# Two-layer hybrid decoder trunk: [high | low] products in the first SwiGLU phase, modulation steps moved to the first mixer, half of the depthwise conv on GpSimd

## The chip, the cores and the metric

The kernel runs on one core of a Trainium2 chip. The metric is device time in microseconds (us) of one execution; lower is better. Engines are called as in the profile: PE is the matrix engine, PEld its weight loads, DVE the vector engine, ACT the scalar engine, POOL is GpSimd, and SP issues most DMAs.

## The reference

Two layers work on x of 256 positions by 1024 channels, all in float32. A vector c gives nine modulation vectors of 1024 per layer.

```python
for l in range(2):
    mod = silu(c) @ ada_w[l] + ada_b[l]           # 1024 -> 9 * 1024
    sh1, sc1, gt1, sh2, sc2, gt2, sh3, sc3, gt3 = split(mod, 9)
    h = rms(x) * (1 + sc1) + sh1
    x = x + 0.5 * gt1 * swiglu(h, ffn1_w_in[l], ffn1_w_out[l])      # 1024 -> 2 * 2816 -> 1024
    P = (rms(x) * (1 + sc2) + sh2) @ mix_w_in[l]
    # attention (8 heads of 64), conv branch, gated linear attention (4 heads of 64)
    o_b = silu(group_layernorm(depthwise_conv31(a * sigmoid(g)) + b))   # 256 channels, causal
    x = x + gt2 * (concat(o_a, o_b, o_c) @ mix_w_out[l])
    h = rms(x) * (1 + sc3) + sh3
    x = x + 0.5 * gt3 * swiglu(h, ffn2_w_in[l], ffn2_w_out[l])
```

## The kernel before

Everything is kept transposed: channels on the 128 partitions, the 256 positions along the free axis. The program is a sequence of phases, named (layer, sub-layer): (0,0), (0,1), (0,2), (1,0), (1,1), (1,2). Sub-layers 0 and 2 are the SwiGLUs (`ffn`), 1 is the mixer (`mix`). A scheduler orders each engine's instructions when the program is built; on the chip each engine runs its list in order.

**Weights.** Each weight piece is 1 MB. `split` loads it into one of five `raw` buffers, ACT copies it to a rounded high part `wh`, and DVE subtracts to get the low part `wl` (lines 327 and 328); there are six buffers each of `wh` and `wl`, of 1024 columns. The activations are held as a high and a low part too: `hT` has both side by side, and `g` (the SwiGLU's inner result) is built the same way.

**Two forms of a product.** Per 128x128 weight block, `mm3` issues three matmuls of 256 columns: high weights by high activations, high weights by low, low weights by high. `mm2` issues two: high weights by the pair [high | low] in one matmul of 512 columns, and low weights by high. `product` uses `mm3` and leaves its sum in one bank of PSUM for both halves of a piece. `product2` uses `mm2`, needs one bank per half, and adds the two column halves outside PE: an ACT copy (line 524) and a DVE addition (line 525) per half. In `ffn` the flag `pairs` selects `product2` in all SwiGLU phases but (0,0). Of the 22 input pieces of (0,0), three are done in `open_first` and 19 by `product`; each has 16 blocks.

**Modulation.** `ada_w` is 72 loads of 1 MB. A step takes one of them: in mode "dve", DVE multiplies it by a column of silu(c) and accumulates (lines 230, 232); in mode "pe", PE multiplies it directly (line 223). When the eight steps of a group of 16 vectors of 128 are done, `ada_sum` adds over partitions on PE (line 251), and `ada_finish` transposes (line 263), adds the bias and forms the scale and gate columns. `PLAN[phase] = (m, tensor, lo, hi)` spreads m steps over the pieces lo to hi of a phase; `AT_END[phase]` adds steps in mode "pe" near the phase's end. Modulation loads share the five `raw` buffers with the weights, and SP issues both from one queue. The opening of (0,0) does the first eight steps; the groups that follow are 16 to 31 (gate 1, shift 2), 32 to 47 (scale 2, gate 2) and 48 to 63 (shift 3, scale 3).

**Conv.** `conv_steps` in `mix` is a generator: each `yield` follows one of the 31 taps, and `taps(n)` is called between the steps of the attention so that the taps lie between other DVE work. A tap is one DVE instruction for each 128 channels (t = 0, 1), accumulating into `y` (lines 732, 735). When all taps are done, a matmul (line 740) begins the group norm. The two POOL memsets of `acaus` (line 898) come later in program order.

`unit` hands out one of 24 buffers of 2 KB per partition, from which most activations come.

Of the kernel before, what the change touches and what calls it, by code (L numbers as in the profile page):

```python
# [44 lines left out]
TAPS = (4, 2, 4, 4, 4, 4)  # L45
ORDER = (0, 2, 6, 4)

PLAN = {None: (0, 0, 0, 1), (0, 0): (22, 0, 0, 30), (0, 1): (0, 0, 0, 1), (0, 2): (19, 0, 5, 28), (1, 0): (15, 0, 5, 28),
        (1, 1): (0, 0, 0, 1), (1, 2): (4, 0, 2, 14)}
AT_END = {(0, 0): 1, (0, 1): 1, (0, 2): 1, (1, 0): 1, (1, 1): 0, (1, 2): 0}  # L50
HOOKS = {(0, 1): (0, 1), (0, 2): (0, 1), (1, 0): (0, 1), (1, 1): (0, 1), (1, 2): (0, 1)}
# [8 lines left out]
def trunk_kernel(ctx: ExitStack, tc: tile.TileContext, x, c, positions, ada_w, ada_b, ffn1_norm, ffn1_w_in,  # L60
# [487 lines left out]
    def ffn(l, i, w_in, w_out, done, first=None):  # L548
# [2 lines left out]
        gT = []  # L551
        ws = []

        pairs = (l, i) != (0, 0)

        def piece(n, ahead=0):

            while len(ws) <= min(n + ahead, KF - 1):
                m = len(ws)
                ws.append(split(wi[:, :, m % 2, T * (m // 2):T * (m // 2) + T], [KD, T], fine=m < 2))  # L560
            return ws[n]
# [14 lines left out]
        for ch in range(KF // 2):  # L576
            if (l, i) == (0, 0) and ch in (2, 6):
                next(tables_rope)
            if (l, i, ch) == (0, 2, 3):
                use_small(1, *load_small(1))  # L580
            if first is not None and ch < 2:
                if ch == 0:
                    continue
                pb = product(piece(3))
                opened, bias = first[4:]
                b = bias()
                for s in range(2):
                    act(opened[0][:, s, :], opened[0][:, s, :], AF.Silu, bias=b[:, s:s + 1])
                    DVE.scalar_tensor_tensor(opened[0][:, s, :], opened[1][:, s, :], b[:, 2 + s:3 + s],
                                             opened[0][:, s, :], op0=ALU.add, op1=ALU.mult)  # L590
                gated(opened[0])
                a = opened[2]
                for s in range(2):
                    act(a[:, s, :], a[:, s, :], AF.Silu, bias=b[:, 4 + s:5 + s])
                DVE.tensor_mul(a, a, pb)
            elif ch == 0:
                (a, ba), (b, bb) = rms(pps[0]), rms(pps[1])
                wh, wl = piece(2)
                pp = [wide(), wide()]
                for k in range(KD):  # L600
                    for s in range(2):
                        cs = P * s, P * s + P
                        mm3(pp[s][:, 0:T + 2], wh(k, *cs), wl(k, *cs), hT[:, k, 0, :], hT[:, k, 1, :], k == 0,
                            k == KD - 1)
                third = rms(pp)
                piece(3)
                modulated(l, i)
                for s in range(2):
                    act(a[:, s, :], a[:, s, :], AF.Silu, bias=ba[:, s, :])
                    DVE.scalar_tensor_tensor(a[:, s, :], b[:, s, :], bb[:, s, :], a[:, s, :], op0=ALU.add,  # L610
                                             op1=ALU.mult)
            else:
                if ch == 1:
                    a, ba = third
                    for s in range(2):
                        act(a[:, s, :], a[:, s, :], AF.Silu, bias=ba[:, s, :])
                elif pairs:
                    a = product2(piece(2 * ch))
                    act(a, a, AF.Silu)
                else:  # L620
                    a = unit([P, 2, T], F32, "ab")
                    act(a, product(piece(2 * ch)), AF.Silu)
                DVE.tensor_mul(a, a, (product2 if pairs else product)(piece(2 * ch + 1)))  # L623
            gated(a)
        wo = w_out[l].rearrange("(k p) n -> p k n", p=P)
        late = []
# [50 lines left out]
    def mix(l, done):  # L677
# [47 lines left out]
        def conv_steps():  # L725

            y = tv
            for k in range(CK):
                for t in range(2):
                    w = cw[l][:, 2 * k + t:2 * k + t + 1]  # L730
                    if k == 0:
                        DVE.tensor_scalar(y[:, t, :], hpad[:, t, 0:T], w, cols[l][:, R_CB + t:R_CB + t + 1],
                                          op0=ALU.mult, op1=ALU.add)
                    else:
                        DVE.scalar_tensor_tensor(y[:, t, :], hpad[:, t, k:k + T], w, y[:, t, :], op0=ALU.mult,  # L735
                                                 op1=ALU.add)
                yield
            pm = bank()
            for t in range(2):
                PE.matmul(pm[:, T * t:T * t + T], grpb, y[:, t, :], start=True, stop=True)  # L740
            DVE.tensor_sub(y, y, pm.rearrange("p (a b) -> p a b", a=2))
            ACT.activation(tg, y, AF.Square)
            bc = group_rstd(tg)
            DVE.tensor_mul(y, y, bc)
            table("silu_and_others")
            for t in range(2):
                act(y[:, t, :], y[:, t, :], AF.Silu, scale=cols[l][:, R_CG + t:R_CG + t + 1],
                               bias=cols[l][:, R_CBE + t:R_CBE + t + 1])
                split_out(y[:, t, :], mixed(4 + t))
            yield  # L750
# [408 lines left out]
```

## Time and profile before

| what | value |
|---|---|
| median of 3 runs | 1063.79 us (1062.51 to 1064.71) |
| the profiled execution, its own time | 1062.44 us |
| its span in the trace | 1060.6 us |
| PE busy | 1043.7 us, 98% of the span |
| DVE / ACT / POOL busy | 855.6 / 600.5 / 6.6 us |
| bytes moved | 251.36 MB, 237 GB/s in the mean |

The profiled execution lasts 1.84 us longer than its span; the median of the runs is 1.35 us above it. A busy share is an average over phases that have different limits, and since PE's matmuls are pipelined, a busy PE is not yet a PE at its peak; rows of single stretches are needed to see what sets the time.

### The profile page before, as it was taken

How to read it: one execution, taken by the hardware profiler on the slowest of the kernel's cores; microseconds unless marked ns; L12 is line 12 of the kernel's file. 1: busy time of each engine (PE TensorE's matmuls, PEld its weight loads, DVE VectorE, ACT ScalarE, POOL GpSimd, SP SyncE). 2: the span in 40 equal slices, each digit the busy share in tenths (PEclk: the TensorE clock that was granted, in tenths of full speed). 3: DMA queues.
4: the chain of work that ended last, by engine and by line, in shares of the span. 5: the costliest groups of instructions: out<-in, count | busy, mean ns of one | idle time of the engine just before them, and what ended most of it. 6: DMA issues, size and time to landing. Idle time of an engine off the chain costs nothing.

```text
span 1060.6 us, 17714 instructions
## 1 busy us (share of the span) xinstructions
PE 1043.7 (98%) x6987; PEld 919.3 (87%) x6987; DVE 855.6 (81%) x1430; ACT 600.5 (57%) x1067; POOL 6.6 (1%) x30
## 2 busy tenths in 40 slices
PE   5999999999999999999999999999999999999998
PEld 4799998888888988888889888888988899888887
DVE  3698887979986899998669998865899789976552
ACT  5464454458665865555457565544767577555541
POOL 1000000000000000000000000000000000000000
PEclk8999999999999999999999999999999999999999
DMA  9989999995326469999776998867343436965430
GB/s 315 366 305 353 328 311 310 318 304 170 125 75 207 152 225 344 346 345 328 239 236 200 321 345 297 284 221 237 122 158 120 159 97 226 311 202 172 159 127 20
DMA packets 177587, 251.36 MB, mean 237 GB/s; under 512 B 7372, under 2 KB 156512, under 8 KB 170336
## 3 DMA queue, kind: packets, MB, share of 16 engines
q1 hardware_dynamic: 177272, 250.14, 70.2%
q8 instruction: 55, 0.90, 0.4%
q14 instruction: 28, 0.23, 0.1%
q10 hardware_dynamic: 232, 0.09, 0.0%
HBM read 249.16 MB, written 1.05 MB: 236 GB/s over the span
## 4 chain that ended last, share of the span: by engine, by line
PE 97%; DMA 1%; DVE 1%; ACT 0%; issue 0%; ACTq 0%; DVEq 0%
PE mm L353 36%; PE mm L354 18%; PE mm L347 8%; PE mm L349 7%; PE mm L348 7%; PE mm L702 3%; PE mm L701 2%; PE mm L703 2%; PE mm L954 2%; PE mm L955 2%; PE mm L953 1%; PE tp L223 1%; PE tp L859 1%; PE tp L832 1%; PE tp L251 1%; PE tp L854 1%
## 5 line engine op out<-in xcount | busy, mean ns | idle before, releaser
L328 DVE TENSOR_TENSOR wl<-raw,wh 128x1024 fp32r<-128x1024 f32 (+1 forms) x352 | 391.8, 1128 | 103.0 <-ACT wh L327 97.8
L327 ACT CAST wh<-raw 128x1024 fp32r<-128x1024 f32 (+1 forms) x352 | 338.5, 975 | 186.3 <-PE mm L353 100.3
L353 PE MATMUL mm<-hT,wh 128*128 128x512 f32 x912 | 322.5, 396 | 0.0
L354 PE MATMUL mm<-hT,wl 128*128 128x256 f32 x912 | 256.0, 281 | 0.0
L353 PE MATMUL mm<-g,wh 128*128 128x512 f32 x704 | 249.3, 398 | 0.0
L353 PEld LDWEIGHTS mm<-hT,wh 128*128 128x128 f32 x912 | 172.3, 189 | 43.0 <-DVE ab L525 1.7
L354 PE MATMUL mm<-g,wl 128*128 128x256 f32 x704 | 197.6, 281 | 0.0
L347 PE MATMUL mm<-hT,wh 128*128 128x256 f32 (+1 forms) x656 | 187.3, 286 | 1.7 <-ACT hT L432 1.5
L349 PE MATMUL mm<-hT,wl 128*128 128x256 f32 (+1 forms) x656 | 187.1, 285 | 0.0
L348 PE MATMUL mm<-hT,wh 128*128 128x256 f32 (+1 forms) x656 | 186.8, 285 | 0.0
L354 PEld LDWEIGHTS mm<-hT,wl 128*128 128x128 f32 x912 | 171.6, 188 | 0.2
L353 PEld LDWEIGHTS mm<-g,wh 128*128 128x128 f32 x704 | 132.2, 188 | 34.9 <-ACT wh L327 1.7
L354 PEld LDWEIGHTS mm<-g,wl 128*128 128x128 f32 x704 | 133.0, 189 | 0.0
L347 PEld LDWEIGHTS mm<-hT,wh 128*128 128x128 f32 x656 | 124.7, 190 | 5.2 <-ACT hT L432 2.1
L349 PEld LDWEIGHTS mm<-hT,wl 128*128 128x128 f32 x656 | 124.8, 190 | 1.7 <-issue 1.6
L232 DVE SCALAR_TENSOR_TENSOR adaacc<-adaraw,cact,adaacc 128x2048 f32<-128x2048 f32 (+1 forms) x59 | 123.4, 2092 | 2.7 <-DMA adaraw<-in_ada_w_dram 2.6
L348 PEld LDWEIGHTS mm<-hT,wh 128*128 128x128 f32 x656 | 124.5, 190 | 0.7 <-DVE hT L433 0.2
L524 ACT COPY ab<-mm 128x256 f32<-128x256 f32 x114 | 41.7, 371 | 57.5 <-PE mm L354 57.3
L673 ACT CAST g<-ab 128x256 fp32r<-128x256 f32 x88 | 31.7, 404 | 39.5 <-DVE ab L623 39.2
L525 DVE TENSOR_TENSOR ab<-ab,mm 128x256 f32<-128x256 f32 x114 | 46.0, 415 | 9.0 <-ACT ab L524 8.7
L735 DVE SCALAR_TENSOR_TENSOR ab<-hpad,cw,ab 128x256 f32<-128x256 f32 x120 | 50.9, 475 | 0.0
L530 DVE SCALAR_TENSOR_TENSOR xT<-mm,gate,xT 128x256 f32<-128x256 f32 x80 | 34.5, 478 | 19.1 <-PE mm L354 18.8
(216 smaller groups left out, 1110.8 us busy)
## 6 DMA issues: line engine op xcount, KB each, us to landing
raw<-in_ffn_w_in_dram SPq DMA_DIRECT2D x85, 1024.0 KB
adaraw<-in_ada_w_dram SPq DMA_DIRECT2D x72, 1024.0 KB
raw<-in_ffn_w_out_dram SPq DMA_DIRECT2D x32, 1024.0 KB
raw<-in_mix_w_in_dram SPq DMA_DIRECT2D x24, 1024.0 KB
raw<-in_ffn_w_out_dram SPq DMA_DIRECT2D x16, 768.0 KB
raw<-in_mix_w_out_dram SPq DMA_DIRECT2D x8, 1024.0 KB
held<-in_ffn_w_in_dram SPq DMA_DIRECT2D x12, 256.0 KB
xn<-in_x_dram SPq DMA_DIRECT2D x4, 256.0 KB
```

Of the source, the lines that this page charges most:

```text
L232: DVE.scalar_tensor_tensor(part, w, cact[:, k, 0:1], part, op0=ALU.mult, op1=ALU.add)
L327: ACT.copy(hs[-1][:, b:c], raw_at(a + b, a + c))
L328: DVE.tensor_sub(ls[-1][:, b:c], raw_at(a + b, a + c), f32(hs[-1][:, b:c]))
L347: PE.matmul(o, wh, high, start=first, stop=False)
L348: PE.matmul(o, wh, low, start=False, stop=False)
L349: PE.matmul(o, wl, high, start=False, stop=last)
L353: PE.matmul(halves(o), wh, pair, start=first, stop=False)
L354: PE.matmul(o[:, 0:T], wl, pair[:, 0, :], start=False, stop=last)
L524: ACT.copy(t[:, s, :], o[s][:, T:2 * T])
L525: DVE.tensor_add(t[:, s, :], t[:, s, :], o[s][:, 0:T])
L530: DVE.scalar_tensor_tensor(xT[:, d, :], o, gate[l][i][:, d:d + 1], xT[:, d, :], op0=ALU.mult, op1=ALU.add)
L735: DVE.scalar_tensor_tensor(y[:, t, :], hpad[:, t, k:k + T], w, y[:, t, :], op0=ALU.mult, op1=ALU.add)
```

## The change

There are three edits. (1) The phase (0,0) uses `product2` everywhere; `pairs` is gone. (2) The plan of (0,0) has 16 steps in place of 22, and that of (0,1), the first mixer, has 6 in mode "dve" over its pieces 1 to 12; `AT_END` is as before, so the totals at the end of (0,1) agree. (3) In both mixers the taps of the second 128 channels go to POOL, which issues a multiplication into `term` and an addition for each tap; all of them stand in program order at the first tap. `term` is one more buffer from `unit`.

```diff
-PLAN = {None: (0, 0, 0, 1), (0, 0): (22, 0, 0, 30), (0, 1): (0, 0, 0, 1), (0, 2): (19, 0, 5, 28), ...
+PLAN = {None: (0, 0, 0, 1), (0, 0): (16, 0, 0, 30), (0, 1): (6, 0, 1, 12), (0, 2): (19, 0, 5, 28), ...
...
-        pairs = (l, i) != (0, 0)
...
-                pb = product(piece(3))
+                pb = product2(piece(3))
...
-                elif pairs:
+                else:
                     a = product2(piece(2 * ch))
                     act(a, a, AF.Silu)
-                else:
-                    a = unit([P, 2, T], F32, "ab")
-                    act(a, product(piece(2 * ch)), AF.Silu)
-                DVE.tensor_mul(a, a, (product2 if pairs else product)(piece(2 * ch + 1)))
+                DVE.tensor_mul(a, a, product2(piece(2 * ch + 1)))
...
         def conv_steps():
             y = tv
-            for k in range(CK):
-                for t in range(2):
-                    w = cw[l][:, 2 * k + t:2 * k + t + 1]
-                    if k == 0:
-                        DVE.tensor_scalar(y[:, t, :], hpad[:, t, 0:T], w, cols[l][:, R_CB + t:R_CB + t + 1],
-                                          op0=ALU.mult, op1=ALU.add)
-                    else:
-                        DVE.scalar_tensor_tensor(y[:, t, :], hpad[:, t, k:k + T], w, y[:, t, :], op0=ALU.mult,
-                                                 op1=ALU.add)
+            def tap(k, t):
+                return hpad[:, t, k:k + T], cw[l][:, 2 * k + t:2 * k + t + 1]
+            for t, V in ((0, DVE), (1, POOL)):
+                V.tensor_scalar(y[:, t, :], *tap(0, t), cols[l][:, R_CB + t:R_CB + t + 1], op0=ALU.mult, op1=ALU.add)
+            term = unit([P, 2, T], F32, "term")
+            for k in range(1, CK):
+                POOL.tensor_scalar(term[:, k % 2, :], *tap(k, 1), None, op0=ALU.mult)
+                POOL.tensor_add(y[:, 1, :], y[:, 1, :], term[:, k % 2, :])
+            yield
+            for k in range(1, CK):
+                DVE.scalar_tensor_tensor(y[:, 0, :], *tap(k, 0), y[:, 0, :], op0=ALU.mult, op1=ALU.add)
                 yield
```

## Rows read from the trace of the kernel before

**Rows 1.** The page's busy shares, and its chain that ended last.

```profile
PE 1043.7 (98%) x6987; PEld 919.3 (87%) x6987; DVE 855.6 (81%) x1430; ACT 600.5 (57%) x1067; POOL 6.6 (1%) x30
...
PE 97%; DMA 1%; DVE 1%; ACT 0%; issue 0%; ACTq 0%; DVEq 0%
```

**Rows 2.** PE's waits over the whole span, longest first: total us, times, longest.

```profile
PE mm L1055 <- DMA xn<-in_x_dram: 3.6, 2, 3.4
...
PE tp L1099 <- DVE shift L1092: 1.0, 1, 1.0
```

**Rows 3.** Busy time by stretch: stretch, length, PE, PEld, DVE, ACT, POOL, PE clock, DMA.

```profile
425.70:476.50 50.80, 50.80 (x290) 44.15 (x288) 49.12 (x61) 29.43 (x51) 0.00 (x0) 1.00 1.00 350
51.00:160.00 109.00, 109.00 (x913) 108.03 (x911) 96.43 (x122) 58.12 (x88) 0.00 (x0) 1.00 0.94 322
...
246.00:327.00 81.00, 81.00 (x523) 67.86 (x522) 76.60 (x179) 54.14 (x111) 0.00 (x0) 1.00 0.41 133
...
762.00:843.00 81.00, 81.00 (x542) 67.55 (x541) 75.75 (x183) 53.97 (x110) 0.00 (x0) 1.00 0.45 145
```

**Rows 4.** The stretch of three-matmul products, line 349 alone (PE, PEld).

```profile
57.35:126.48 69.13, 54.28 (x192) 36.17 (x192) 1.00 0.96 331
```

**Rows 5.** Stretches of two-matmul products, line 353 alone (PE, PEld).

```profile
162.46:188.90 26.44, 26.39 (x76) 14.10 (x76) 1.00 0.94 309
390.77:419.17 28.40, 28.36 (x80) 15.12 (x80) 1.00 0.94 330
...
425.65:476.56 50.91, 50.87 (x144) 27.19 (x144) 1.00 0.99 349
```

**Rows 6.** Groups by form, whole span: count, busy us, mean ns, idle before.

```profile
L232 DVE SCALAR_TENSOR_TENSOR adaacc<-adaraw,cact,adaacc 128x2048 f32<-128x2048 f32 x45 | 105.5, 2345 | 2.5 <-DMA adaraw<-in_ada_w_dram 2.5
...
L525 DVE TENSOR_TENSOR ab<-ab,mm 128x256 f32<-128x256 f32 x114 | 46.0, 415 | 9.0 <-ACT ab L524 8.7
L524 ACT COPY ab<-mm 128x256 f32<-128x256 f32 x114 | 41.7, 371 | 57.5 <-PE mm L354 57.3
```

**Rows 7.** Line 232 alone in a stretch of (0,0): DVE busy and count.

```profile
51.00:160.00 109.00, 28.14 (x12) 1.00 0.94 322
```

**Rows 8.** PE in order of time at the end of phase (0,2): start, us.

```profile
542.68 1.04 PE L251 MATMUL tp<-adaacc,ones 128*32 128x512 f32 x8
...
548.29 0.28 PE L354 MATMUL mm<-g,wl 128*128 128x256 f32 x1
548.41 0.28 PE L347 MATMUL mm<-hT,wh 128*128 128x258 f32 x1
```

**Rows 9.** DVE in order of time, first mixer: taps, and the operation before line 820.

```profile
248.34 0.73 DVE L732 TENSOR_SCALAR ab<-hpad,cw,cols 128x256 f32<-128x256 f32 x2
...
266.54 0.42 DVE L815 TENSOR_TENSOR tmp<-tmp,tmp 128x256 f32<-128x256 f32 x1
...
307.80 4.42 DVE L735 SCALAR_TENSOR_TENSOR ab<-hpad,cw,ab 128x256 f32<-128x256 f32 x11
```

**Rows 10.** PE in order of time, first mixer: lines 820 and 740.

```profile
267.01 0.66 PE L820 MATMUL tp<-ident,tmp 128*128 128x128 f32 x4
...
337.10 1.13 PE L740 MATMUL tp<-ab,grpb 128*128 128x256 f32 x4
```

**Rows 11.** POOL in order of time.

```profile
3.22 0.30 POOL L125 TENSOR_SCALAR_AFFINE_SELECT gmask<-gmask 128x128 f32<-128x128 f32 x1
3.45 0.53 POOL L129 MEMSET reset<- 128x512 f32 x1
...
226.84 0.99 POOL L898 MEMSET acaus<- 128x512 f32 x2 [221.49 <-PE mm L354]
```

**Rows 12.** Groups of DVE in the first mixer, 246 to 327 us.

```profile
L328 DVE TENSOR_TENSOR wl<-raw,wh 128x1024 fp32r<-128x1024 f32 x23 | 27.5, 1216 | 0.0
L735 DVE SCALAR_TENSOR_TENSOR ab<-hpad,cw,ab 128x256 f32<-128x256 f32 x60 | 25.4, 474 | 0.0
```

**Rows 13.** SP's DMA issues in order of time, first mixer.

```profile
254.10 2.62 SPq L312 DMA_DIRECT2D raw<-in_mix_w_in_dram  x2
```

More of the change, by code (lines that the diff above doesn't have):

```diff
@@ L46 @@
 ORDER = (0, 2, 6, 4)
-PLAN = {None: (0, 0, 0, 1), (0, 0): (22, 0, 0, 30), (0, 1): (0, 0, 0, 1), (0, 2): (19, 0, 5, 28), (1, 0): (15, 0, 5, 28),
+PLAN = {None: (0, 0, 0, 1), (0, 0): (16, 0, 0, 30), (0, 1): (6, 0, 1, 12), (0, 2): (19, 0, 5, 28), (1, 0): (15, 0, 5, 28),
         (1, 1): (0, 0, 0, 1), (1, 2): (4, 0, 2, 14)}
```

## The prediction, made before the change was run

> **What bounds the kernel now.** I read the page's shares first, then PE's waits, then the busy time by stretch. PE is busy for 98% of the span, and the chain that ended last is 97% PE [rows 1]. A busy PE could still be waiting inside that figure, so the second view asks whom it waits for: the longest wait is 3.6 us, for x to arrive at the start, and the next one on the page that the argument meets is 1.0 us, still in the opening [rows 2]. After that PE waits for nobody by more than a fraction of a microsecond, at a granted clock of 1.00, which is the 2.4 GHz level [rows 3]. So time can leave this kernel only where PE gets less to do, and it can enter wherever another engine becomes late for PE. The same view shows where lateness threatens: in the first mixer DVE is busy for 76.60 of the 81 us from 246 to 327, in the second for 75.75 of 81, and in the late pieces of (0,2) for 49.12 of 50.80, in each case under a PE without gaps. DMA is at 0.94 of its engines in (0,0) and at 0.41 in the first mixer [rows 3].
>
> **Edit 1, the products of (0,0).** What changes on PE is only the number of matmuls; the columns are 768 for a block in both forms. The price of each form is read from a stretch with nothing else in it. Between 57.35 and 126.48 us PE does 192 blocks by three matmuls [rows 4]: 69.13 / 192 = 0.3600 us a block. Between 425.65 and 476.56 it does 144 blocks by two [rows 5]: 50.91 / 144 = 0.3535. The difference is 0.0065 us, and 19 pieces of 16 blocks are 304 blocks, so the saving is 304 x 0.0065 = 2.0 us. Two other stretches bound it: 80 blocks in 28.40 us are 0.3550 (saving 1.5 us), and 76 blocks in 26.44 us, the quickest and on the operand g, are 0.3479 (saving 3.7 us) [rows 5]. I take 2.0, since that stretch is the longest and reads hT, as (0,0) will.
>
> The new additions are 38 ACT copies of 0.371 us and 38 DVE additions of 0.415 us [rows 6]: 14.1 us on ACT and 15.8 on DVE. ACT has 58.12 us of work in the 109 us from 51 to 160 [rows 3], so its copies lie beside PE at no cost. DVE has 96.43 there, 12 modulation steps among them [rows 3, 7]. The plan's 16 in place of 22 leaves 12 x 16/22 = 8.7 of these, which takes off 3.3 x 2.345 = 7.7 us [rows 6]. DVE then has 96.4 + 15.8 - 7.7 = 104.5 us of work in 109 - 2 = 107 us, 98%. The stretch in (0,2) has 49.12 / 50.80 = 97% with PE full [rows 3], so I cost this at nothing; without that cover, what DVE has above 107 us would come onto PE, and an underestimate of 5% would be 3 us. The two PSUM banks of a piece in place of one are what (0,2) has as well, in that same gapless stretch.
>
> **Edit 2, six modulation steps moved.** Each is a load, a wait of DVE for it, and 2.345 us on DVE [rows 6]. The six loads leave (0,0), where DMA is nearly full, but PE waits there for no DMA [rows 2], so nothing is gained. In the mixer they add 6.3 MB to 133 GB/s x 81 us = 10.8 MB, or 211 GB/s, against 350 GB/s that the late pieces of (0,2) reach [rows 3]. On SP each load stands between weight loads and holds one of the five buffers; the mixer's last two projection loads are issued at 254.10 us [rows 13], some 50 us ahead of PE's use of them, and six turns of a buffer among eighteen do not use that up. Cost nothing. On PE the counts stay the same: one step by PE at the end of (0,0) and one at the end of the mixer, before and after. What moves is which group is finished where: with 16 steps, group 32 to 47, with the scale that the mixer's first operand needs, is finished only at the end of (0,0). The end of (0,2) has just this order already: the summing on PE (1.04 us) at 542.68 and the next phase's first matmul at 548.41, 0.12 us behind the matmul ahead of it [rows 8]. So no gap is expected; at most a microsecond or two if hT comes late.
>
> **Edit 3, half of the conv to POOL.** DVE sheds one tap of 128 channels 31 times in each mixer. Back to back they start every 4.42 / 11 = 0.40 us [rows 9], so 12.4 us go. In the first mixer 6 x 2.345 = 14.1 us come in their place: 76.6 + 1.7 = 78.3 of 81 us, still inside. In the second mixer DVE is relieved by 12.4 us, but PE has no wait there to give back, so this is worth nothing.
>
> POOL gets 61 operations per mixer. The trace has no such operation on POOL, so its price is bounded. Below: a memset of 512 columns takes 0.53 us [rows 11], which is 0.27 for 256; nothing below that is likely, as the new ones also read. Above: a select of 128 columns, which reads one operand, takes 0.30 [rows 11]; for 256 columns that is 0.60 with one operand and, doubled again, 1.20 with two. The chain is 16.5 us at the low end, 31 x 0.60 + 30 x 1.20 = 54.6 at the high one; I take 0.60 for all, nearest to the select, 36.6 us. It starts at 248.3 [rows 9] and the norm's matmul wants it at 337.1 [rows 10], so POOL has 88.8 us, 1.46 us for each operation, before it is late. The memsets for acaus were issued at 226.84 [rows 11], before the conv; behind the chain they would come at 285 to 303, ahead of the norm. Cost nothing.
>
> What the trace can't show is DVE and POOL reading the same memory at the same time: POOL does nothing but write between 5 us and the end. If the two run freely, the cost is 0. If one holds up the other, the upper bound is POOL's whole chain. By the first the sum for both mixers is 0; the second is the main rival below. I take 0 for the forecast, as no row shows the interference, and keep the other for the range. The Trainium skill speaks against this choice: by SBUF — State Buffer, "Who interferes with whom", a VectorE instruction with two operands in SBUF and a GpSimd instruction that reads SBUF need the same read interface, and the one that comes second waits until the first is done. By that rule the sum would be the rival's; no run here shows it yet, as POOL's later instructions only write.
>
> **The sum.** 1062.44 (the profiled execution) - 2.0 = 1060.4; the median of the runs is 1.35 higher, so on its scale 1063.79 - 2.0 = **1061.8 us**. The bounds of the product's price make it 1060.1 to 1062.3. A change below 0.2% (2.1 us) is about what measurements of this kernel can't tell from none, so the forecast lies on that edge.
>
> **Rivals.** *(A) The forecast*: PE's saving of 1.5 to 3.7 us and nothing else, chance 0.52; 0.29 of it beyond 0.2%, 0.23 within.
>
> *(B) POOL's reads and DVE's exclude each other, and DVE becomes the bound of the first mixer.* About three quarters of DVE's time there is work with two operands in that memory (the 27.5 us of the weight splits, what is left of the 25.4 us of taps [rows 12], the modulation steps). At POOL's low price DVE loses 0.75 x 16.5 = 12.4 us, against 81 - 76.6 = 4.4 us of idle time. PE has next to no lead over DVE in places: line 820 starts at 267.01, and the DVE operation before it ends at 266.54 + 0.42 = 266.96 [rows 9, 10]. So the excess, 8 us, goes to PE. The second mixer has 5.25 us idle and the 12.4 us it was relieved of, so it stands this. Time 1061.8 + 8 = 1070 us. At 0.60 an operation the loss is 27.5 us in each mixer, 23 beyond the idle time in the first and 10 in the second: 1095 us. It decides from (4.4 + 2.0) / 61 = 0.10 us of DVE lost per POOL operation. For it: both engines will read the same buffers, for 40 us, in a stretch where DVE is 95% busy. Against it: the price per operation may be mostly fixed cost, in which POOL reads nothing, and POOL itself may be the one that waits, with 88.8 us to spare. Chance 0.31.
>
> *(C) DVE's order becomes late in single places*: a modulation step of 2.345 us stands ahead of a short operation that PE waits for, where a tap of 0.40 us stood; or (0,0) overflows; or hT comes late in the mixer's opening. Six steps at up to 2 us are 12 us at the very most; one or two of them count, so +1 to +4 on the forecast, 1063 to 1066 us. Against it: the modulation steps in (0,2) are of the same length, and PE doesn't wait there. Chance 0.09, 0.02 of it within 0.2%.
>
> *(D) More than the forecast*: the quick price of 0.3479 holds and a fraction of the mixers' small waits goes too, 1059 to 1060 us. Against it: neither stretch on hT was that quick [rows 5]. Chance 0.08.
>
> **How the numbers follow.** Faster by over 0.2%: 0.29 + 0.08 = 0.37. Within: 0.23 + 0.02 = 0.25. Slower: 0.31 + 0.07 = 0.38. Both signs hold much of the chance, so the forecast's own range stands beside: 1060.1 to 1062.3. The range for 8 in 10 goes from 1059 (the lower end of D, with little below it) to 1074 us; above that lies the dearer half of B, about 0.15.
>
> **What would show it.** In the profile after, the blocks of (0,0) should come every 0.353 us without a gap, with line 524 and 525 counted 152 times in place of 114, and DVE near 98% there. The mixers should last as long as before. POOL should show 61 operations a mixer, with the last before line 740's matmul. Wrong would be: durations of DVE operations in the mixers that are longer than before by tenths of a microsecond while POOL runs (B); PE waiting for DVE at line 820 or in the attention (B, C); PE waiting for line 525's sums in (0,0) (C); or POOL's last addition just ahead of line 740 (a price near 1.46 us).

## The result, and the profile after

The changed kernel takes 1092.17 us (median of 4 runs, 1090.96 to 1092.65) against 1064.17 of the kernel before on the same chips: ratio 1.0259, 95% interval 1.0247 to 1.0271. It is 28 us slower; the forecast was 2 us faster. The profiled span went from 1060.6 to 1089.2 us.

The page's busy shares of the kernel after, and its chain that ended last (beside [rows 1]):

```profile
PE 1052.7 (97%) x6683; PEld 907.7 (83%) x6683; DVE 874.8 (80%) x1406; ACT 614.6 (56%) x1105; POOL 159.4 (15%) x152
...
PE 82%; DVE 13%; ACT 2%; issue 2%; DMA 1%; ACTq 0%; DVEq 0%
```

304 matmuls went and PE's busy time rose. The chain is the better reader: DVE had 1% of it and now has 13%. So whom does PE wait for? PE's waits over the whole span, after:

```profile
PE tp L820 <- DVE tmp L815: 7.2, 3, 4.0
...
PE tp L820 <- DVE tmp L817: 3.6, 4, 1.1
...
PE mm L347 <- ACT hT L479: 3.2, 1, 3.2
PE tp L854 <- ACT tmp L851: 2.5, 4, 0.9
```

None of these was among the waits before [rows 2]; these four lie in the mixers. Busy time by stretch, after (columns as in [rows 3]); the first two are windows of that group, the third is POOL's chain in the second mixer, the fourth what follows it:

```profile
246.00:327.00 81.00, 73.66 (x429) 59.73 (x428) 80.56 (x136) 46.25 (x89) 78.17 (x61) 0.98 0.56 182
...
762.00:843.00 81.00, 73.95 (x433) 61.63 (x432) 77.09 (x140) 49.49 (x97) 65.10 (x55) 0.98 0.44 141
777.00:851.00 74.00, 66.98 (x385) 54.75 (x384) 71.81 (x129) 43.47 (x84) 72.82 (x62) 0.98 0.43 138
851.00:913.00 62.00, 61.26 (x522) 55.62 (x521) 40.92 (x97) 40.21 (x88) 0.69 (x2) 1.00 0.37 125
```

In the second mixer DVE lost half of its taps and got no steps, and while POOL's chain runs it is busy for 71.81 of 74 us; PE works on 433 matmuls in the window where it worked on 542. Behind POOL's chain DVE falls to 40.92 of 62; part of that fall is the mixer's own, since before the change its last 62 us were lighter too (49.86 of DVE). That POOL's chain holds the mixer back is so far a reading, which the experiments test.

DVE's groups of 246 to 327 us, after, beside [rows 12]; and POOL's own over the whole span:

```profile
L328 DVE TENSOR_TENSOR wl<-raw,wh 128x1024 fp32r<-128x1024 f32 x19 | 26.1, 1377 | 0.0
L736 DVE SCALAR_TENSOR_TENSOR ab<-hpad,cw,ab 128x256 f32<-128x256 f32 x24 | 14.9, 621 | 0.0
...
L813 DVE TENSOR_TENSOR tmp<-mm,rope 128x512 f32<-128x512 f32 x4 | 2.7, 675 | 0.0
...
L815 DVE TENSOR_TENSOR tmp<-tmp,tmp 128x256 f32<-128x256 f32 x4 | 2.4, 601 | 0.0
```

```profile
L732 POOL TENSOR_SCALAR term<-hpad,cw 128x256 f32<-128x256 f32 x60 | 89.8, 1506 | 0.0
L733 POOL TENSOR_TENSOR ab<-ab,term 128x256 f32<-128x256 f32 x60 | 61.6, 1027 | 2.4
```

The last two of DVE's groups, in the same window before:

```profile
L813 DVE TENSOR_TENSOR tmp<-mm,rope 128x512 f32<-128x512 f32 x4 | 2.7, 679 | 0.0
L815 DVE TENSOR_TENSOR tmp<-tmp,tmp 128x256 f32<-128x256 f32 x4 | 1.7, 415 | 0.0
```

A weight split takes 1377 ns in place of 1216, a tap 621 in place of 474, line 815 takes 601 in place of 415. The operation with `mm`, a PSUM operand, is no longer than before (675 against 679). Now each DVE operation of a stretch is counted at its own duration, and once more at the mean that operations of its kind have in the kernel before: those that start between 243.0 and 324.4 us, while POOL's first chain runs, sum to 91.1 us where they would have summed to 76.2; in the second chain (776.9 to 850.8 us) 80.4 against 66.9; behind it (851 to 913 us) 46.7 against 46.8. So POOL's 61 operations take some 14 us from DVE in each mixer (14.9 and 13.5), 0.23 us each, and the half conv gave it 12.4.

**Where the 28.6 us of span lie.** A mixer is measured from its first three-matmul product (line 347) to the first two-matmul product (line 353) of the next phase, in PE's order of time, so that the next phase's opening counts with it; the mixer's own opening ends at the last matmuls of line 769, the gate's weights, some 21.5 us into it. Before: the mixers begin at 226.96 and 740.64 us and take 146.5 and 143.7. After: 226.51 and 757.18, and they take 163.4 (+16.9) and 155.8 (+12.1). What lies ahead is 0.45 us shorter, the rest within 0.2 us. In the second mixer PE is idle for 7.8 us in place of 0.3, and its mean granted clock is 0.989 in place of 1.00, which over 155.8 us is worth up to 1.7 us (less where PE was idle anyway); in the first it is idle for 11.6 us at a clock of 0.979, worth up to 3.4.

### The profile page after: what moved, and what is told of

Its sections match the earlier page's. It is cut to its first block, busy times and chain, and to the rows that moved or that the text cites. A ratio compares the mean times of both kernels' runs of the same rounds, so it can differ in the third digit from the quotient of the medians.

```text
span 1089.2 us, 17237 instructions
## 1 busy us (share of the span) xinstructions
PE 1052.7 (97%) x6683; PEld 907.7 (83%) x6683; DVE 874.8 (80%) x1406; ACT 614.6 (56%) x1105; POOL 159.4 (15%) x152
## 4 chain that ended last, share of the span: by engine, by line
PE 82%; DVE 13%; ACT 2%; issue 2%; DMA 1%; ACTq 0%; DVEq 0%
PE mm L353 41%; PE mm L354 21%; DVE wl L328 3%; PE mm L347 3%; PE mm L348 3%; PE mm L349 3%; DVE ab L736 2%; PE mm L953 1%; PE mm L955 1%; PE mm L954 1%; PE tp L223 1%; ACT wh L327 1%; PE tp L251 1%; DVE ymod L471 1%; DVE adaacc L232 1%
## 5 line engine op out<-in xcount | busy, mean ns | idle before, releaser
L328 DVE TENSOR_TENSOR wl<-raw,wh 128x1024 fp32r<-128x1024 f32 (+1 forms) x352 | 398.5, 1144 | 109.4 <-ACT wh L327 103.0
L353 PE MATMUL mm<-hT,wh 128*128 128x512 f32 x1216 | 430.4, 397 | 0.0
L354 PE MATMUL mm<-hT,wl 128*128 128x256 f32 x1216 | 341.8, 281 | 0.0
L353 PEld LDWEIGHTS mm<-hT,wh 128*128 128x128 f32 x1216 | 229.8, 189 | 57.8 <-DVE ab L525 1.7
L353 PEld LDWEIGHTS mm<-g,wh 128*128 128x128 f32 x704 | 132.2, 188 | 34.6 <-ACT wh L327 2.5
L354 PEld LDWEIGHTS mm<-g,wl 128*128 128x128 f32 x704 | 133.0, 189 | 0.0
L347 PE MATMUL mm<-hT,wh 128*128 128x258 f32 (+1 forms) x352 | 102.7, 293 | 4.9 <-ACT hT L479 3.2
L348 PE MATMUL mm<-hT,wh 128*128 128x258 f32 (+1 forms) x352 | 101.6, 290 | 0.8 <-DVE hT L480 0.8
L349 PE MATMUL mm<-hT,wl 128*128 128x258 f32 (+1 forms) x352 | 101.7, 289 | 0.0
L524 ACT COPY ab<-mm 128x256 f32<-128x256 f32 x152 | 55.5, 370 | 77.5 <-PE mm L354 77.4
L732 POOL TENSOR_SCALAR term<-hpad,cw 128x256 f32<-128x256 f32 x60 | 89.8, 1506 | 0.0
L347 PEld LDWEIGHTS mm<-hT,wh 128*128 128x128 f32 x352 | 67.9, 194 | 7.6 <-ACT hT L479 3.7
L525 DVE TENSOR_TENSOR ab<-ab,mm 128x256 f32<-128x256 f32 x152 | 61.5, 416 | 11.0 <-ACT ab L524 10.3
L348 PEld LDWEIGHTS mm<-hT,wh 128*128 128x128 f32 x352 | 68.1, 193 | 2.5 <-DVE hT L480 1.9
L733 POOL TENSOR_TENSOR ab<-ab,term 128x256 f32<-128x256 f32 x60 | 61.6, 1027 | 2.4
```

The lines of the kernel that those rows point to most:

```text
L328: DVE.tensor_sub(ls[-1][:, b:c], raw_at(a + b, a + c), f32(hs[-1][:, b:c]))
L347: PE.matmul(o, wh, high, start=first, stop=False)
L348: PE.matmul(o, wh, low, start=False, stop=False)
L349: PE.matmul(o, wl, high, start=False, stop=last)
L353: PE.matmul(halves(o), wh, pair, start=first, stop=False)
L354: PE.matmul(o[:, 0:T], wl, pair[:, 0, :], start=False, stop=last)
```

## The experiments

| kernel | time, us | ratio to before (95%) | mixer 1: opening + rest | mixer 2 |
|---|---|---|---|---|
| before | 1063.8 to 1065.3 | 1 | 21.5 + 125.0 | 143.7 |
| after | 1092.17 | 1.0259 (1.0247 to 1.0271) | 27.6 + 135.8 | 155.8 |
| e3_pool_alone | 1088.77 | 1.0218 (1.0203 to 1.0233) | 21.5 + 136.6 | 155.8 |
| half_left_out | 1069.61 | 1.0040 (1.0025 to 1.0055) | 26.1 + 125.0 | 145.4 |
| pool_writes_only | 1072.18 | 1.0067 (1.0049 to 1.0085) | 26.5 + 126.0 | 147.2 |
| pool_mults_only | 1076.57 | 1.0116 (1.0097 to 1.0134) | 27.2 + 128.1 | 148.4 |
| pool_adds_only | 1094.12 | 1.0279 (1.0259 to 1.0300) | 30.3 + 135.5 | 157.7 |
| e1_products_alone | 1069.99 | 1.0051 (1.0037 to 1.0066) | 26.2 + 126.7 | 143.7 |
| e2_steps_alone | 1075.32 | 1.0093 (1.0076 to 1.0110) | 27.3 + 132.2 | 143.7 |
| e12_conv_on_dve | 1073.80 | 1.0084 (1.0067 to 1.0101) | 26.1 + 131.4 | 143.7 |
| e13_no_steps | 1093.26 | 1.0262 (1.0246 to 1.0278) | 27.1 + 135.4 | 155.8 |
| late_steps_18 | 1071.59 | 1.0061 (1.0048 to 1.0074) | 22.5 + 133.0 | 143.7 |
| after_ymod_first | 1096.85 | 1.0306 (1.0292 to 1.0321) | 23.6 + 142.2 | 155.9 |
| e1_ymod_first | 1067.50 | 1.0027 (1.0015 to 1.0038) | 21.9 + 129.0 | 143.8 |
| e12_ymod_first | 1073.72 | 1.0088 (1.0074 to 1.0103) | 23.5 + 132.9 | 143.8 |

Four texts, the first three and that of micro_ports, name their theories by letters. L: POOL's reads and DVE's two-operand work exclude each other. M: the six steps overload DVE and POOL is innocent. O: the engines' lists were ordered for a lighter DVE and are tight for that reason.

**Edit 3 alone, and everything but edit 3.**

```diff
 e3_pool_alone: before, with only
+            for t, V in ((0, DVE), (1, POOL)):
+                V.tensor_scalar(y[:, t, :], *tap(0, t), ...)
+            ... POOL.tensor_scalar(term...); POOL.tensor_add(y[:, 1, :], ...)
 e12_conv_on_dve: after, with the conv loop of before
```

> The kernel before with the second half of the conv on POOL and nothing else (edit 3 alone). Theory L: both mixers are longer, the second by the 12 us that it had in the changed kernel, the first by somewhat less than 16.9 since the six steps are not there, some 8 to 13; total 1084 to 1089 us. The weight splits in the mixers take 1.30 to 1.36 us in place of 1.216. Theory M: only the second mixer is longer, by 12 at most, total 1064 to 1076, the first as before. Theory O: both longer by about 12, but the durations of DVE's operations are as before.

> The changed kernel with the whole conv back on DVE (edits 1 and 2 without 3). Theory L (POOL's reads and DVE's two-operand work exclude each other): no DVE operation is stretched, the taps take 0.474 us again; the second mixer (from its first matmul to the next phase's first two-matmul product) is back from 155.8 to 143.7 us; the first has 14.1 us more DVE work than before and 4.4 us of idle time, so it gives back most of its 16.9 us but keeps up to 10. Total 1062 to 1072 us. Theory M (the six modulation steps overload DVE, POOL is innocent): the first mixer keeps its whole 16.9 us, total about 1079, and the second mixer's 12 us stay unexplained. Theory O (the list of each engine was reordered for a lighter DVE and is tight for that reason): both mixers go back, total 1062.

Edit 3 alone lengthens the mixers by 11.6 and 12.1 us, which is 23.7 of the 28. Without it the second mixer is back at 143.7 to a tenth and the first still 11.0 longer. The losses of the two edits together, 11.6 + 11.0 = 22.6, are more than the 16.9 of the full change: with half of the taps gone, the steps find more room. L's range holds for edit 3 alone; without edit 3 the first mixer kept 1 us more than L allows, and the time lies 1.8 us above its range. M is ruled out by edit 3 alone, which has no moved step and loses in both mixers.

**The second 128 channels left out.** Taps 1 to 30 of them are left out, tap 0 is DVE's; POOL has no conv.

```diff
-            for t, V in ((0, DVE), (1, POOL)):
-                V.tensor_scalar(y[:, t, :], *tap(0, t), ...)
+            for t in range(2):
+                DVE.tensor_scalar(y[:, t, :], *tap(0, t), ...)
-                POOL.tensor_scalar(term...); POOL.tensor_add(...)
```

> The changed kernel with 30 taps of the second 128 channels left out, so that neither POOL nor DVE does them (only tap 0 remains, on DVE; the output lacks that part of the conv). DVE's own list in the mixers is as long as in the changed kernel. Theory L: without a reader on POOL nothing is stretched; the second mixer is at 143 to 144 us and the first near 147 to 149; total 1062 to 1064 us. Theory M: the first mixer keeps 16.9 us, total 1079. Theory O: the second mixer keeps about 12 us, since the lists are built for the same light DVE; total 1075 or more.

POOL's chain thus costs 163.4 - 151.1 = 12.3 us and 155.8 - 145.4 = 10.4 us. O would have kept some 12 us in the second mixer and is out; L's ranges for this kernel were missed as well, the mixers being 2.1 and 1.4 us longer than they allow. With POOL silent DVE's splits and taps take 1220 and 481 ns, so neither the shorter list nor a chain of taps in one `y` half stretches them. Two more things are read here. Taking 12.4 us of work from DVE made the second mixer no shorter than before (145.4 against 143.7; the 1.7 us are not explained). And the first mixer's rest is 125.0, exactly as before, with four of the six steps in it (of the other two, one runs 10 us ahead of the mixer, at 217.9 us, and one in its opening): behind the opening, relief and steps cancel, as the prediction's balance had it. There the relief is worth something, since with the whole conv on DVE the same steps leave a rest of 131.4. The 4.6 us that remain lie in the opening.

**Which of POOL's operations.** In the first, constants are written in place of the conv half; in the second the additions, in the third the products are left out.

```diff
 pool_writes_only
-  POOL.tensor_scalar(term...); POOL.tensor_add(y[:, 1, :], ...)
+  POOL.memset(term, 1.0); POOL.memset(term, 0.5); POOL.memset(y[:, 1, :], 1.0)
 pool_mults_only
-  POOL.tensor_add(y[:, 1, :], y[:, 1, :], term[:, k % 2, :])
 pool_adds_only
-  POOL.tensor_scalar(term...); POOL.tensor_add(y[:, 1, :], y[:, 1, :], term[:, k % 2, :])
+  POOL.tensor_add(y[:, 1, :], y[:, 1, :], hpad[:, 1, k:k + T])
```

> As the changed kernel, but for the second 128 channels of the conv, which are left out: in their place GpSimd writes constants, 60 times into the buffer for the product (both halves of it, 512 columns) and 31 times into the 256 columns of the sum, so that it is at work through the same stretch of either mixer and reads nothing. VectorE has the first 128 channels alone, as in the changed kernel. Theory reads (GpSimd's reads of SBUF take turns with VectorE's): the mixers are as long as with the second half left out, 151.1 and 145.4 us, the time is 1069.6 us within 1.5, and the two row operations ahead of the transposes that TensorE waits for (L814, L815) are back near 0.42 us. Rival activity (any work of GpSimd holds VectorE up, its writes too, or its late memsets for the softmax mask do): the mixers are near 163.4 and 155.8 us and the time is above 1085 us.

> As the changed kernel, but GpSimd makes only the 30 products of a mixer and never adds them to the sum: the additions are left out, so the second 128 channels hold tap 0 alone. Theory price by operation (beside each other in the measurement by itself an addition of two operands cost VectorE some 0.32 us and a multiplication some 0.09): of the 12.3 and 10.4 us that GpSimd's chain costs the two mixers, the products carry 0.09 of 0.41, that is 2.7 and 2.3 us: mixers near 153.8 and 147.7 us, the time near 1074.6 us. Rival by GpSimd's time (the loss goes with how long GpSimd is at work; the products took 89.8 of 151.4 us of it): 7.3 and 6.2 us, mixers 158.4 and 151.6 us, the time near 1083 us.

> As the changed kernel, but GpSimd makes only the 30 additions of a mixer, of the unscaled window of the padded input to the sum: the products are left out. Theory price by operation: the additions carry 0.32 of 0.41, that is 9.6 and 8.1 us: mixers near 160.7 and 153.5 us, the time near 1087.3 us. Rival by GpSimd's time (the additions took 61.6 of 151.4 us): 5.0 and 4.2 us, mixers 156.1 and 149.6 us, the time near 1078.8 us.

DVE's splits and taps of 246 to 327 us, in that order of kernels:

```profile
L328 DVE TENSOR_TENSOR wl<-raw,wh 128x1024 fp32r<-128x1024 f32 x21 | 25.5, 1219 | 0.3 <-ACT wh L327 0.3
L737 DVE SCALAR_TENSOR_TENSOR ab<-hpad,cw,ab 128x256 f32<-128x256 f32 x30 | 14.4, 480 | 0.0
```

```profile
L328 DVE TENSOR_TENSOR wl<-raw,wh 128x1024 fp32r<-128x1024 f32 x20 | 24.5, 1230 | 0.4 <-ACT wh L327 0.4
L735 DVE SCALAR_TENSOR_TENSOR ab<-hpad,cw,ab 128x256 f32<-128x256 f32 x30 | 15.0, 500 | 0.0
```

```profile
L328 DVE TENSOR_TENSOR wl<-raw,wh 128x1024 fp32r<-128x1024 f32 x19 | 25.5, 1344 | 0.0
L734 DVE SCALAR_TENSOR_TENSOR ab<-hpad,cw,ab 128x256 f32<-128x256 f32 x21 | 12.6, 598 | 0.0
```

Writing, POOL is busy for 41 us in each mixer (31.6 + 31.6 + 19.1 us for both) and DVE's durations are those of before. With products they are 1 and 5% longer, with additions 11 and 26%. Summed as above, DVE's loss is 0.5 to 0.7 us a mixer beside the writes, 3.6 beside 30 products (0.12 each) and 12.8 and 11.3 beside 30 additions (some 0.4 each). In time, over half_left_out: writes +1.4 and +1.8 us in the two mixers, products +4.2 and +3.0, additions +14.7 and +12.3. The additions of two operands in SBUF make most of the loss; the price by operation holds against the price by POOL's time. The size was too low: additions alone cost more than the pair, which starts an addition only every 2.7 us. That excess (2.4 and 1.9 us over the full change) goes with PE's clock in the trace: with additions alone its mean granted share is 0.959 and 0.968 in the two mixers in place of 0.979 and 0.989, worth up to 3.4 us more in each, while PE's idle time is 11.9 and 8.9 us against 11.6 and 7.8. Why the clock stays lower for longer wasn't tried. The writes came out 1 us above the range that was given for them; in the second mixer their 1.8 us are likewise the size of what the clock costs there (0.988, up to 1.7).

**The two engines by themselves.** A kernel without the trunk, run once: 30 taps of DVE in a chain beside 30 operations of POOL, 128 x 256 each.

```diff
+ for k in range(30): DVE.scalar_tensor_tensor(accd, src[:, k:k + 256], w, accd, ...)   # or ps, in PSUM
+ for k in range(30): POOL.tensor_add(accp, accp, term)        # or tensor_scalar, or memset
```

> No trunk at all: rows of 30 DVE operations of the tap's form (128x256, one pointer scalar) with 30 POOL operations beside them, section by section; the output is only x passed through. Theory L: alone a tap starts every 0.40 us (30 in 12 us). Beside POOL's additions and multiplications, which read, 30 taps take 12 us plus a good part of POOL's own time, so 20 to 35 us; beside POOL memsets, and with DVE's large operand in PSUM, they stay at 12 to 14 us. POOL alone: 0.3 to 0.9 us for a multiplication, 0.6 to 1.1 for an addition; beside DVE operations of 2048 columns, 2.3 us each, POOL's become several times as long. Rivals to L (POOL has no influence, the stretch is from elsewhere): every section of taps takes 12 to 14 us.

DVE in order of time (start, us): 25 taps beside products, 30 beside additions, 30 with POOL almost idle. The last were to run beside writes, but POOL's writes stand earlier in its order (16.9 to 46.1 us), so this kernel doesn't test them.

```profile
92.07 14.24 DVE L109 SCALAR_TENSOR_TENSOR accd<-src,w,accd 128x256 f32<-128x256 f32 x25
...
122.07 25.26 DVE L114 SCALAR_TENSOR_TENSOR accd<-src,w,accd 128x256 f32<-128x256 f32 x30
...
149.47 15.79 DVE L119 SCALAR_TENSOR_TENSOR accd<-src,w,accd 128x256 f32<-128x256 f32 x30
```

A tap starts every 0.526 us alone (15.79 / 30), 0.570 beside products, 0.842 beside additions. Groups of the same kernel, with the taps that read `ps` in PSUM:

```profile
L116 POOL TENSOR_TENSOR accp<-accp,term 128x256 f32<-128x256 f32 x30 | 23.5, 785 | 2.4
L126 POOL TENSOR_TENSOR accp<-accp,term 128x256 f32<-128x256 f32 x30 | 21.7, 722 | 2.4
L131 POOL TENSOR_TENSOR accp<-accp,term 128x256 f32<-128x256 f32 x30 | 21.7, 722 | 2.3
L124 DVE SCALAR_TENSOR_TENSOR accd<-ps,w,accd 128x256 f32<-128x256 f32 x30 | 14.5, 484 | 1.1
L134 DVE SCALAR_TENSOR_TENSOR accd<-ps,w,accd 128x256 f32<-128x256 f32 x30 | 14.5, 484 | 1.1
```

Beside additions (L124) such a tap takes 484 ns as it does alone (L134), and the additions 722 (L126) where they take 785 beside taps from SBUF (L116). Both readers have to want SBUF. Some 29 additions ran beside the 30 taps, so one costs DVE about (25.26 - 15.79) / 29 = 0.32 us; it loses only 0.06 us itself. Beside long DVE operations it is POOL that waits. Its product of line 96 in order of time, beside DVE operations of 2048 columns and with DVE idle:

```profile
79.80 2.77 POOL L96 TENSOR_SCALAR accp<-psrc,gate 128x256 f32<-128x256 f32 x1
...
191.84 0.92 POOL L96 TENSOR_SCALAR accp<-psrc,gate 128x256 f32<-128x256 f32 x1
```

An addition takes 2.65 us there in place of 0.72, while the long operation takes 2.69 in place of the 2.345 of [rows 6]. The Trainium skill's SBUF — State Buffer, "Who interferes with whom", has this rule: a VectorE instruction with two inputs in SBUF contends with a GpSimd instruction that reads SBUF, and not with one that only writes. The trace agrees on the operands, and pool_writes_only on the writes, whose DVE durations are those of before. So theory L holds for the additions (25.26 us for 30 taps), for the long operations, and for PSUM in that nothing is stretched. Two sizes were missed: a tap alone starts every 0.526 us and not every 0.40, and beside products 30 taps take some 17 us where 20 to 35 were expected.

**Edit 1 alone, edit 2 alone, edits 1 and 3, and later steps.**

```diff
 e1_products_alone: after, with the plan and the conv of before
 e2_steps_alone: before, with the plan of after
 e13_no_steps: after, with the plan of before
 late_steps_18: e12_conv_on_dve, with
-PLAN (0, 0): (16, 0, 0, 30), (0, 1): (6, 0, 1, 12)
+PLAN (0, 0): (18, 0, 0, 30), (0, 1): (4, 0, 11, 15)
```

> Edit 1 alone: the first phase's products in pairs, the plan of the modulation and the conv as before. Theory kept (304 blocks at 0.3532 us in place of 0.3600, and VectorE's 112 us of work in the stretch of (0,0) still lie inside it because it has idle time ahead of the phase's end and TensorE's products don't need the added halves at once): the stretch of (0,0) is 174.2 us, the mixers 146.5 and 143.7 us as before, the time 1062.4 us, 1.8 below before. Rival (with all 22 modulation steps left in the phase VectorE is its bound): VectorE ends (0,0) late, TensorE waits for it there, the gain is eaten and the time is 1064 to 1070 us.

> Edit 1, the conv on VectorE as before, and only four modulation steps moved out of the first phase, placed in the first mixer's last pieces (from piece 11 on, where VectorE has idle time in the profile of before), not in its first twelve. Theory room (what the moved steps cost is VectorE's want of idle time in the first two thirds of the mixer, and the last third has it): the first mixer is within 1.5 us of 146.5, the time is 1062 to 1064 us. Rival (the mixer has no room for steps anywhere): four of the six steps' 11.0 us, 7.3 us, come back, the first mixer is near 154 us and the time near 1070 us.

> Edit 2 alone: six modulation steps to the first mixer, products of the first phase and conv as before. Theory sums (the first mixer has 4.4 us of idle VectorE ahead of its end and 14.1 us of new work): the first mixer is 9.7 us longer, near 156 us, the time near 1073.5 us. Rival difference (the six steps cost what lies between edits 1 and 2 together and edit 1 alone, 157.5 less 152.9 us): 4.6 us, the mixer near 151.2 us, the time near 1068.8 us.

> Edits 1 and 3 without edit 2: GpSimd has the second 128 channels of the conv and the plan is the one of before. Theory VectorE (what edit 1 leaves to VectorE at the end of the first phase costs the first mixer 6.4 us on top of the 11.6 us of GpSimd's chain): the first mixer is 163 to 165 us, the second 155.8 us, the time 1092 to 1095 us. Rival relief (GpSimd's half gives VectorE the room for that, and the 5.3 us that the first mixer lost beyond GpSimd's 11.6 are the six steps'): the first mixer is 158 to 160 us and the time 1087 to 1089.5 us.

Neither edit 1 nor edit 2 pays by itself, and what each costs appears in the first mixer. With edit 1 alone, four splits of 512 columns more than before start inside the mixer, 4 x 0.69 = 2.7 us of DVE left over from a full (0,0); the mixer is 6.4 longer, 4.7 of it in its opening. The time is within the rival's range, but by another way: inside (0,0) PE waits for DVE only once, for 0.6 us. With edit 2 alone the mixer is 13.0 longer, more than the sum of work (9.7) and far more than the difference of 4.6: the rival fell. Part of the 13.0 is PE's clock, whose mean share there is 0.957, worth up to 6.8 us; PE is idle for 7.7. Without the steps the full change keeps 16.0 of its 16.9 us there, with an opening of 27.1 us (rival relief fell; theory VectorE had the time, and the mixer half a us too long); so edit 1's leftover costs as much in the opening as the steps do. The two don't add: in the full change two splits of 512 columns fewer than before start inside the mixer, so the leftover is gone once the steps leave (0,0). The late pieces had no room either: four steps between 299 and 343 us leave the opening nearly whole (22.5), and the rest pays 8.0 us, 3.5 of it in one wait of PE for the attention's `tmp`.

**The opening's order.** DVE in order of time at the start of the first mixer, after:

```profile
233.06 0.15 DVE L379 TENSOR_TENSOR rs_t<-rs_y 128x2 f32<-128x2 f32 x1
233.13 2.35 DVE L232 SCALAR_TENSOR_TENSOR adaacc<-adaraw,cact,adaacc 128x2048 f32<-128x2048 f32 x1
235.39 0.15 DVE L380 TENSOR_TENSOR rs_t<-rs_t,rs_v 128x2 f32<-128x2 f32 x1
...
238.71 1.23 DVE L328 TENSOR_TENSOR wl<-raw,wh 128x1024 fp32r<-128x1024 f32 x1 [1.59 <-ACT wh L327]
239.86 1.41 DVE L466 TENSOR_TENSOR ab<-mm,rsb 128x256 f32<-128x256 f32 x4
241.18 0.87 DVE L471 SCALAR_TENSOR_TENSOR ymod<-xT,acol,rsb 128x256 f32<-128x256 f32 x2
```

A step of 2.35 us stands between two operations of 0.15 us of the norm, then a split waits for ACT, then come four operations of line 466; the modulated input (line 471) starts 14.7 us into the mixer. Before, it started 10.5 us into it, ahead of line 466. Busy time by stretch there, after:

```profile
237.00:242.00 5.00, 2.38 (x20) 2.17 (x19) 3.41 (x9) 4.49 (x13) 0.00 (x0) 1.00 0.92 345
242.00:247.00 5.00, 4.47 (x19) 3.93 (x20) 4.95 (x10) 1.89 (x5) 4.01 (x4) 0.66 0.38 95
```

PE waits 3.2 us, and behind the wait the granted clock is 0.66 over 5 us, that is the 1.2 GHz level for some 3.4 us, which costs half of it, 1.7. Together 4.9 of the opening's 6.1 us. Does the order of lines 466 and 471 make them?

```diff
+        if l == 0: modulated(l, 1)
         tg, bg = rms(pps[0])
         tv, ba = rms(pps[1])
-        modulated(l, 1)
+        if l: modulated(l, 1)
```

> The changed kernel with one call moved: in the first mixer the modulated input (the products with the norm's scale, line 471, and their split, lines 479 and 480) is asked for ahead of the two openings' sums (line 466), so that VectorE's order has two products of line 471 before the four of line 466, as before the change. Theory order (some 5 of the first mixer's 16.9 us come from VectorE's order in its opening: behind line 466 the modulated input is late, TensorE waits 3.2 us for it and its clock falls behind that): the first mixer is within 1.5 us of 158.1, its length with GpSimd's half of the conv alone, the second stays at 155.8 us, and the time is 1086 to 1088.5 us. Rival backlog (VectorE is late there because of the moved steps' work, whatever its order): the first mixer stays above 162 us and the time above 1090 us.

> Edit 1 alone, with the same call moved in the first mixer. Theory order: the 4.9 us that the first mixer lost in its opening with edit 1 alone come back, the first mixer is 147 to 149.5 us in place of 152.9, and the time is 1064.5 to 1067 us. Rival backlog (all 22 steps inside the first phase leave VectorE behind when the mixer begins): the mixer stays above 151.5 us and the time above 1068.5 us.

> Edits 1 and 2 with the conv on VectorE as before, with the same call moved in the first mixer. Theory order: 4.6 to 5.4 of the first mixer's 11.0 us come back, the other 6 are the price of the six steps beside a full conv: mixer 151.5 to 153.5 us, time 1067.5 to 1070 us. Rival backlog: the mixer stays above 156 us and the time above 1072.5 us. A third way, that the six steps cost nothing once the order is restored: mixer under 149 us and time under 1066 us.

Theory order holds for the opening and fails for the time: the full change and edits 1 and 2 came out in the rival's ranges, edit 1 alone between the two. The openings are 4.0, 4.3 and 2.6 us shorter, and the granted clock stays at 1.00 in 242 to 247 us in all three. But the rest grew by 6.4, 2.3 and 1.5 us. Only edit 1 alone keeps 2.5 us of the time; the full change became 4.7 slower. What comes earlier in the opening mostly waits later; that DVE has no room there is argued and was not tested apart. Why the full change lost more than it had gained stays open. No kernel of the study beats the one before.

## Why the prediction was wrong, point by point

**Edit 3, the interference taken as 0: the step that failed.** No row showed it, both bounds stood in the text, and the lower one was taken; the runs show 14 us of DVE's time lost in each mixer. The other bound, POOL's whole chain, is far off too: beside 73.9 us of chain in the second mixer DVE lost 13.5. Rival B had the mechanism, and the measured loss lies near its low price of 12.4; its threshold of 0.10 us per operation was passed with 0.23. Yet B's time at that price was 1070 us, and 1092 came. That B's dearer time of 1095 us is close is luck: it goes by a loss of 27.5 us a mixer, twice the measured one. The line of B that fails is "The second mixer has 5.25 us idle and the 12.4 us it was relieved of, so it stands this". 17.65 us of room did not hold a loss of 13.5: the mixer lost 12.1. half_left_out shows one half of the reason: in that mixer the relief was worth nothing to PE. The other half is read from the order of time: the taps are what DVE does between operations that PE waits for, and the loss falls on those operations too. DVE in order of time ahead of the longest wait, and PE at its end:

```profile
273.43 0.68 DVE L813 TENSOR_TENSOR tmp<-mm,rope 128x512 f32<-128x512 f32 x1
274.03 0.63 DVE L379 TENSOR_TENSOR rs_t<-rs_y 128x16 f32<-128x16 f32 x1
274.58 1.21 DVE L328 TENSOR_TENSOR wl<-raw,wh 128x1024 fp32r<-128x1024 f32 x1
275.72 0.69 DVE L380 TENSOR_TENSOR rs_t<-rs_t,rs_v 128x16 f32<-128x16 f32 x1
276.33 0.41 DVE L814 TENSOR_TENSOR tmp<-tmp,tmp 128x256 f32<-128x256 f32 x1
...
276.75 0.62 DVE L815 TENSOR_TENSOR tmp<-tmp,tmp 128x256 f32<-128x256 f32 x1
```

```profile
277.43 1.12 PE L820 MATMUL tp<-ident,tmp 128*128 128x128 f32 x4 [3.99 <-DVE tmp L815]
```

Two operations of 16 columns (lines 379 and 380) take 0.63 and 0.69 us, where the mean was 0.18 and 0.17 before, and line 815 takes 0.62 in place of 0.42 [rows 9]. The prediction itself had read that PE has no lead there [rows 9, 10]; it then balanced averages. Its reading of PE's waits [rows 2] also passed over four of 1.1 to 3.2 us in the opening and one of 1.0 us behind it; no term rests on these.

**POOL's price** was mis-sized: 1.51 us for a product and 1.03 for an addition in place of 0.60, so the chain took 81.4 us in place of 36.6. It still ended ahead of the conv's norm, at 324.4 against 352.7 us. With VectorE idle the two take 0.92 and 0.72 us (micro_ports); the rest is read as the contention, the other way round.

**Edit 1** was right on PE. In 58.61 to 149.02 us of after, 512 matmuls are 256 blocks at 90.41 / 256 = 0.3532 us, with no gap, and the phase from its first whole product to the mixer is 1.8 us shorter, where 2.0 was said. "I cost this at nothing", for DVE at 98%, was wrong: with edit 1 alone, what DVE can't finish there hardly stops PE in (0,0); the next phase pays, with 6.4 us, 4.7 of them in its opening. (After the full change DVE was busy for 102.38 of the 109 us from 51 to 160, 94%.) And the first whole product starts 1.3 us later than before, so that the mixer begins only 0.45 earlier. The kernels of this study that share this first phase start that product anywhere from 52.3 to 54.3 us, so the gain of 1.8 is no larger than this scatter; where the scatter comes from isn't settled.

**Edit 2** at nothing: wrong by the opening, right behind it. Beside a halved conv without POOL's chain the rest of the mixer is unchanged; beside a full one the steps cost 13.0 us. In the opening this looks like the mechanism of rival C, a step of 2.35 us ahead of operations of 0.15, with its size at 4.6 to 6.1 where 1 to 4 was said; that step was not moved alone, and edit 1's leftover makes an opening as long without it.

## What to carry to other kernels

GpSimd is not a free engine beside a busy VectorE: an addition of two SBUF operands took 0.3 to 0.4 us from VectorE, and moving half of the taps off, 0.40 us each, in two operations each lost some 14 us where it gave 12.4. Room in an engine is counted at the operations that the bound engine waits for, and not as idle time over a stretch: where that engine waited for nothing, 12.4 us of relief were worth nothing, while a loss of 13.5 us that fell on short operations too cost 12.1. Where an engine has no lead at the start of a phase, look at what the phase before leaves it and which long operation stands ahead of the first short one.

## What the runs showed of the hardware

A GpSimd product by a scalar operand from SBUF (0.92 us) was slower than its addition of two tensors (0.72), and yet the addition was the one that held VectorE up more (0.4 us against 0.12 in the mixers). Beside VectorE operations of 2048 columns GpSimd's addition took 2.65 us. GpSimd's writes left VectorE's durations as they were (a split 1219 ns against 1216), and VectorE's operations with an operand in PSUM were untouched (675 ns against 679, and 484 with and without additions beside them). Taps of one dependent chain start every 0.526 us; two chains in turn, as before the change, every 0.40.
